# Sums of three weight quads moved into the last pair's attention, x's tiles loaded ahead on another queue, one pair's outputs kept in SBUF

## The chip, the cores and the metric

The kernel runs on one core of a Trainium2 chip. The metric is device time of one execution in microseconds; the median of several runs is given. The engines are named as in the profile: PE (TensorE, matrix products; PEld is its weight load), DVE (VectorE), ACT (ScalarE), POOL (GpSimd) and SP (SyncE, which only issues transfers). Transfers are issued on SP's, ACT's or POOL's queue, and each queue issues in its own order: what waits at its head holds what stands behind it. Accumulating transfers (`accum_op=ALU.add`) are all issued by POOL here.

## The reference

One decoder layer, 1024 tokens by 1024 features, all in float32:

```
proj = rms_norm(h, g1) @ w_in
a_b, a_c, a_h, q, k, v, c_u, c_v = split(proj)
y_a = a_b * short_conv(a_c * a_h)                     # width 256
y_b = stick_breaking_attention(norm(q), norm(k), v)   # 8 heads of 64
y_c = spatial_gating(gelu(c_u), gelu(c_v))            # width 256
h = h + concat(y_a, y_b, y_c) @ w_out
f = square(relu(rms_norm(h, g2) @ w_ff1))             # 1024 x 4096
h = h + f @ w_ff2
h = h + sigmoid(rms_norm(h, g3) @ w_ple_gate) * (p @ w_ple_proj)
```

## The kernel before

**Layout.** Activations are kept transposed, features on the 128 partitions, tokens along the row, in two halves of 512 tokens. Each float32 operand of a matrix product is split into a high and a low part (`split`, L135: a rounding copy on ACT, L138, and a subtraction on DVE, L139), and each product is three matmuls (L165 to L167; L772 in the later stages): high times high, high times low, low times high. SBUF tiles of 128 x 512 come from a pool of 56 slots (`slot`) and from smaller pools of the later stages (`late_slot`: 4 tiles "raw", 6 "sum", 22 "w", 12 "tmp").

**Order.** The program text doesn't fix the order in which instructions go into an engine's queue. A planner makes it when the program is built: it plays the program through with a timing model and issues on each engine what is ready, earlier text first. `with tc.issue_after(x)` only forbids that what stands in the block is queued ahead of `x` on x's engine. At run time each engine works in the order of its queue and waits on semaphores.

**Stages.** First come the projections, the spatial gating and the attention. The eight heads are worked in four pairs (`attend(pr)`, eight steps each: a head of the pair and a group of 256 queries; `stick` makes the weights, `gather` turns them and multiplies by v). Beside a pair's attention `weave` runs a stream of other products: the projections of the next pairs, and in the last pair the convolution (`convolve`), whose last part is left for after the attention. In `stick`, POOL multiplies the weights of query blocks 0, 1, 2, 4 and 6 (L429), DVE the others; `last_pool` and `last_act` name the latest such instruction on POOL and the latest sigmoid on ACT. In `convolve`, POOL scales u (L603) and the sum (L613), and DVE evicts the last product from PSUM (L615).

The attention's outputs of pairs 0 to 2 go to HBM (`y_dram`, rows 0 to 2). The last pair's are gathered in two tiles `y_b`, each stored to row 3 when it is full (L490). The gating's outputs are rows 4 and 5; the convolution's stay in SBUF (`y_a`, rows 6 and 7). `bring(0)` loads and splits the rows of the first token half ahead of the next stage; the second half's are loaded within it.

**The stage of w_out** (L879 to L928) runs over two token halves and eight row blocks each, in the order 0, 4, 1, 5, 2, 6, 3, 7. Each block is 24 matmuls into a PSUM bank `o_ps`. Its weights come as two loads "raw" on SP's queue (except in the first two blocks, whose weights are brought early); x's tile `xt` follows on SP's queue (L898; the last two by `fetch`). DVE adds the product to x (L758), ACT's queue stores the sum (`h_dram`), ACT scales it by the gain (L911, `hg`) and squares it (L845), and the squares are added up, in the first half on POOL (L758), in the second by an accumulating transfer (L849). The scaled sums are split as operands `hn` of the next stage. The root of the first half's mean square goes over DVE (`diag`, L866) to PE (`R_ps`, L873).

**The first feed-forward product** multiplies 2 x 2 blocks by seven products in place of eight. Its weights are 16 quads of blocks A11, A12, A21 and A22 (each 128 x 512 floats), and needs four sums of each: S1 = A21 + A22, S2 = A11 + S1, S3 = A11 + A21, S4 = A12 + S2. For quads 3 to 15 these are made in SBUF as the stage goes. For the first three (`EARLY`) they are made in HBM, in `u_sums`, in twelve steps, four for each quad (`block_step`, L745): in step 0 S1 and S3 get a copy of a block, in step 1 S1 gets A22 added and S2 a copy of A11, in step 2 S3 gets A21 and S2 gets S1 added, in step 3 S4 gets a copy of A12 and then S2 added. Copies are issued on ACT's queue (L752), additions on POOL's (L750). The twelve steps stand in the stage of w_out, one for each block whose squares are added up (`up_sums`), queued behind that addition and behind the scaling L911. SP's queue loads the sums from `u_sums` in the second half of the stage.

The weights of the second feed-forward product are summed likewise, in `w_sums`, in 32 steps over the four pairs' attention (`block_sums`, L287); in the last pair only one transfer of these is left. The rest of the kernel, both feed-forward products and the gate, the change doesn't touch.

Of the kernel before, what the change touches and what calls it, by code (L numbers as in the profile page):

```python
# [7 lines left out]
F32 = mybir.dt.float32  # L8
F32R = mybir.dt.float32r
AF = mybir.ActivationFunctionType  # L10
# [22 lines left out]
def hybrid_block(ctx: ExitStack, tc: tile.TileContext, a: dict):  # L33
# [39 lines left out]
    def halves(s, dt=F32, shape=(P, HT)):  # L73
        return [slot(s, dt, shape) for _ in range(2)]
# [212 lines left out]
    def block_sums(i, behind):  # L287


        with tc.issue_after(behind[0].ins), tc.issue_after(behind[1].ins):  # L290
            for to, what in PASSES[i % 4]:
# [12 lines left out]
                else:  # L304
                    nc.scalar.dma_start(w_sums[to, rows], src[rows])

    last_pool, last_act = [None], [None]
    summed = []
    heads = {}
    y_dram = dram.tile([6, 2, P, HT], F32, name="y_dram")  # L310

    def project(pr):
# [77 lines left out]
    def attend(pr):  # L390

        QS, KH, KL, V, _ = heads[pr]
        yb = halves("y_b") if pr == 3 else None
        weights, both, seen_g = {}, [None], []

        def store_rows():
# [39 lines left out]
        def gather(hh, g):  # L436
            own = slice(hh * HD, (hh + 1) * HD)
            wts = weights.pop((hh, g))
            av_of[0] ^= 1
            av = av_bank[:, av_of[0] * 256:(av_of[0] + 1) * 256]  # L440

            def turn(j):

                tr = bank(ps_tr, "w_tr")
                n = 0
                parts = []
                for kb in (2 * j, 2 * j + 1):
                    first = 0 if kb <= 2 * g else 1
                    parts.append((kb, n, first))
                    for i in range(first, 2):  # L450
                        nc.tensor.transpose(tr[:, n:n + P], wts[i][:, kb * P:(kb + 1) * P], ident)  # L451
                        n += P
                hi, lo = tmp("wT_hi", F32R), tmp("wT_lo", F32R)
                split(tr[:, :n], hi[:, :n], lo[:, :n])
                return parts, hi, lo, n // P

            turned = []
            for j in range(-2, g + 1):
                if j + 2 <= g:
                    turned.append(turn(j + 2))  # L460
                    yield 2 * turned[-1][3] + 10
                if j < 0:
                    continue
                parts, hi, lo, _ = turned.pop(0)
                for kb, o, first in parts:
                    m = 256 - first * P
                    lhs = V[kb // 2][:, kb % 2, hh].rearrange("p two d -> p (two d)")
                    for part in (hi, lo):
                        nc.tensor.matmul(av[:, first * P:], lhs, part[:, o:o + m],  # L469
                                         start=kb == 0 and part is hi,  # L470
                                         stop=kb == 2 * g + 1 and part is lo)
                yield 8

            if yb is None:
                if both[0] is None:
                    both[0] = slot("y_both")
                t = both[0]
                nc.scalar.copy(t[:, (g % 2) * 256:(g % 2 + 1) * 256], av)
                if len(seen_g) % 2:
                    nc.gpsimd.dma_start(t[:HD], t[HD:], accum_op=ALU.add)  # L480
                    summed.append((y_dram[pr, g // 2, own], t))
                    both[0] = None
                seen_g.append(g)
                return
            low = half_tmp("av_lo")
            nc.scalar.copy(low[:HD], av[HD:])
            nc.vector.tensor_tensor(out=yb[g // 2][own, (g % 2) * 256:(g % 2 + 1) * 256],
                                    in0=av[:HD], in1=low[:HD], op=ALU.add)
            if hh == 1 and g % 2 == 0:
                nc.sync.dma_start(y_dram[pr, g // 2], yb[g // 2])  # L490

        steps = [(0, g) for g in range(4)] + [(1, g) for g in reversed(range(4))]
        yield from stick(*steps[0])
        for i, step in enumerate(steps):
            if i + 1 < len(steps):
                yield from stick(*steps[i + 1])
            block_sums(8 * pr + i, (last_pool[0], last_act[0]))
            yield from gather(*step)
            if i % 2 == 1:
                store_rows()  # L500
# [155 lines left out]
        weave(attend(pr), ATTEND, fill, PROJECT if pr < 3 else CONVOLVE * 0.72)  # L656
    y = [[], []]

    def bring(h):

        i = len(y[h])
        src = stage(y_dram[i, h]) if i < 6 else y_a[i - 6][h]
        y[h].append(pair("y"))
        split(src, *y[h][-1])

    def early_units(src):

# [9 lines left out]
    for i in range(7):  # L677
        bring(0)
        if i in (2, 4):
            first_wu[2 * i - 4] = early_units(a["w_out"][2 * i - 4])  # L680
        for _ in take(fill, CONVOLVE * 0.28 / 7):
            pass
    for _ in fill:
        pass
    bring(0)
# [42 lines left out]

    OPERAND = {1: "A11", 2: "A12", 4: "A22", 5: "S1", 6: "S2", 7: "S3", 3: "S4"}

    def w_block(key, of, *at):
        return a[key][(2 * (int(of[1]) - 1) + int(of[2]) - 1, *at)]

    def down_operand(p, c, j):
        of = OPERAND[p]
        if of[0] == "A":
            return w_block("w_ff2", of, c, j)
        s = w_sums[int(of[1]) - 1].rearrange("r n -> (r n)")
        return s.rearrange("(c j p n) -> c j p n", j=4, p=P, n=2 * HT)[c, j]


    STEPS = [((0, "A21"), (2, "A11")), ((0, "+A22"), (1, "A11")), ((2, "+A21"), (1, "+S1")),
             ((3, "A12"), (3, "+S2"))]

    def block_step(step, sums, blocks, copies):  # L745
        for to, what in STEPS[step]:
            of = what.strip("+")
            src = sums(int(of[1]) - 1) if of[0] == "S" else blocks(of)
            if what[0] == "+":
                nc.gpsimd.dma_start(sums(to), src, accum_op=ALU.add, max_dma_last_dim=2048)  # L750
            else:
                copies.dma_start(sums(to), src)  # L752

    def subtract(eng, out, x, y):
        return eng.tensor_tensor(out=out, in0=x, in1=y, op=ALU.subtract)
# [23 lines left out]
    UP = (1, 6, 5, 7, 2, 3, 4)  # L779
    FIRST = (1, 2, 6, 5, 7, 3, 4)  # L780
    raw_of, up_pairs = {}, {}

    EARLY = 3
    u_sums = dram.tile([EARLY, 4, P, HT], F32, name="u_sums")

    def up_sums(i, behind_add, behind_act):

        if i < 4 * EARLY:
            with tc.issue_after(behind_add.ins), tc.issue_after(behind_act.ins):
                block_step(i % 4, lambda to: u_sums[i // 4, to],  # L790
                           lambda of: w_block("w_ff1", of, i // 4), nc.scalar)

    def load_up(q, to, of):
        tag = "sum" if to[0] == "S" else "raw"
        src = u_sums[q, int(of[1]) - 1] if of[0] == "S" else w_block("w_ff1", of, q)
# [80 lines left out]
    def hn_pair(src):  # L876
        return two_parts(src, lambda s: slot(f"hn_{s}", F32R))

    last_sqs, up_step = [], [0]  # L879
    late_bank("pass"), late_bank("pass")  # L880
    for h in range(2):
        for n in (0, 4, 1, 5, 2, 6, 3, 7):
            end = h == 1 and n in (3, 7)
            if h == 1:

                if n == 5:
                    with tc.issue_after(block_end.ins):
                        diag = root_of([S2[0]], "20")
                elif n == 6:
                    with tc.issue_after(block_end.ins):  # L890
                        spread_root(diag, R2[0])
                supply({4: -12, 1: -10, 5: -8, 2: -6, 6: -4, 7: -3}.get(n, -100))
            wu = first_wu[n] if h == 0 and n in first_wu else plain_units(a["w_out"][n])
            if end:
                xt = fetch(a["xT"][n * P:(n + 1) * P, half[h]], "sum")
            else:
                xt = slot("xt")
                nc.sync.dma_start(xt, a["xT"][n * P:(n + 1) * P, half[h]])  # L898
            o_ps = late_bank("o_ps")
            block_end = product(o_ps, [(wu[k], y_parts[h][k]) for k in range(KT)])  # L900
            if h == 0:
                i = len(y_parts[1])
                src = fetch(y_dram[i, 1], "sum") if i < 6 else y_a[i - 6][1]
                y_parts[1].append(two_parts(src, lambda s: late_slot("w", f"y_{s}", F32R)))
            if h == 1 and n == 7:
                supply(-0.975)

            evicted = add(nc.vector, xt, o_ps, xt)
            nc.scalar.dma_start(h_dram[n, h], xt)
            t = hg[n][h] = late_slot("tmp", "hg")  # L910
            scaled = nc.scalar.activation(t, xt, AF.Copy, scale=g2[:, n:n + 1])  # L911
            summed = late_squares(S2[h], xt, n == 0, h == 1, end)
            if end:
                last_sqs.append(summed)
            elif summed:
                up_sums(up_step[0], summed, scaled)
                up_step[0] += 1
            if h == 1 and n == 7:
                supply(-0.955)
            j = n % 4  # L920
            if h == 0:
                hn[1 if n < 4 else 2][j] = hn_pair(t)
            elif n >= 4:
                b11, b12, b21 = hg[j][0], hg[j][1], hg[n][0]
                t2 = late_slot("tmp", "t2")
                token_sums(b11, b12, b21, t, nc.vector, b11, t2, b12, b21)
                for p, src in ((6, t2), (5, b11), (7, b12), (3, t), (4, b21)):
                    hn[p][j] = hn_pair(src)  # L928
# [374 lines left out]
```

## Time and profile before

| | us |
|---|---|
| median of 3 runs (1233.39 to 1236.79) | 1236.44 |
| the profiled execution | 1236.95 |
| its span, from the first instruction to the last | 1234.4 |
| PE busy in the span | 1201.2 |
| DVE busy | 885.5 |
| ACT busy | 627.4 |
| POOL busy | 393.3 |

Times in the profile count from the start of the span. The last pair's attention with the convolution beside it runs from about 345 us to 424.7, the stage of w_out from there to about 530, the first feed-forward product to about 840, the second to about 1147, and then the gate. The page cuts the span into 40 slices of 30.9 us; a digit is the busy share in tenths. A matmul's end is modelled, so a busy PE can still run at half its clock; the granted clock stands in a column of its own. A wait is put down to the instruction whose end released it.

### The profile page before, as it was taken

The numbers are of one execution on the slowest core, as the hardware profiler recorded it, in microseconds if no ns is written. First come the engines' busy times: TensorE is split into PE (matmuls) and PEld (weight loads), VectorE is DVE, ScalarE is ACT, GpSimd is POOL, SyncE is SP. The second block draws the span as 40 slices with busy tenths as digits, with TensorE's granted clock in tenths as the row PEclk, the third lists the DMA queues.
The fourth block names the chain that finished last, engine by engine and source line by source line (L and its number), as shares of the span: only waits on it lengthen the run. The fifth ranks groups of instructions, "written<-read, shape, count | busy, mean of one in ns | idle before, by whom it ended". The sixth has DMA issues, their size and how long they took to land.

```text
span 1234.4 us, 17751 instructions
## 1 busy us (share of the span) xinstructions
PE 1201.2 (97%) x5852; PEld 1027.2 (83%) x5852; DVE 885.5 (72%) x1310; ACT 627.4 (51%) x1244; POOL 393.3 (32%) x408
## 2 busy tenths in 40 slices
PE   9999999999999998899999999999999999999997
PEld 7899899898988787688888888888888888888886
DVE  7746888879689654787787777777755566753597
ACT  7726666667565353553433433445544344555552
POOL 2324345355222222215445345331013211013412
PEclk9999999999999998999999999999999999999999
DMA  9602359998621378989999998868969985653957
GB/s 315 217 18 101 113 164 263 244 188 148 129 70 35 116 236 251 265 240 242 267 254 239 259 265 224 255 206 283 363 212 306 298 257 183 200 180 104 185 158 211
DMA packets 128539, 255.08 MB, mean 207 GB/s; under 512 B 14560, under 2 KB 22496, under 8 KB 127744
## 3 DMA queue, kind: packets, MB, share of 16 engines
q1 hardware_dynamic: 97584, 172.80, 42.1%
q0 software_dynamic: 27664, 57.05, 24.7%
q10 hardware_dynamic: 3200, 24.12, 5.3%
q8 instruction: 46, 0.75, 0.3%
q14 instruction: 45, 0.37, 0.1%
HBM read 192.83 MB, written 93.32 MB: 232 GB/s over the span
## 4 chain that ended last, share of the span: by engine, by line
PE 84%; DVE 6%; DMA 4%; issue 2%; ACT 2%; POOL 1%; SPq 0%; ACTq 0%; DVEq 0%; POOLq 0%
PE f_ps L772 25%; PE d_ps L772 25%; PE g_ps L772 6%; PE qkv_ps L165 3%; PE qkv_ps L166 3%; PE qkv_ps L167 3%; DMA xt<-in_xT 2%; PE av L469 2%; DVE rem L426 2%; PE w_tr L451 2%; PE cv_ps L165 1%; PE cv_ps L166 1%; PE cv_ps L167 1%; PE vu_ps L167 1%; PE vu_ps L165 1%
## 5 line engine op out<-in xcount | busy, mean ns | idle before, releaser
L139 DVE TENSOR_TENSOR w_lo<-raw,w_hi 128x512 fp32r<-128x512 f32 x280 | 239.8, 860 | 83.5 <-ACT w_hi L138 80.8
L138 ACT CAST w_hi<-raw 128x512 fp32r<-128x512 f32 x280 | 171.5, 619 | 230.0 <-PE d_ps L772 106.8
L772 PE MATMUL f_ps<-hn_hi,w_hi 128*128 128x512 f32 x448 | 175.5, 393 | 0.0
L772 PE MATMUL f_ps<-hn_lo,w_hi 128*128 128x512 f32 x448 | 175.3, 391 | 0.0
L772 PE MATMUL f_ps<-hn_hi,w_lo 128*128 128x512 f32 x448 | 175.0, 391 | 0.0
L772 PE MATMUL d_ps<-f_hi,w_hi 128*128 128x512 f32 x448 | 174.8, 390 | 0.0
L772 PE MATMUL d_ps<-f_hi,w_lo 128*128 128x512 f32 x448 | 174.3, 389 | 0.0
L772 PE MATMUL d_ps<-f_lo,w_hi 128*128 128x512 f32 x448 | 174.3, 389 | 0.0
L426 DVE TENSOR_TENSOR_SCAN rem<-rem 128x128 f32<-128x128 f32 (+3 forms) x64 | 91.7, 1438 | 19.5 <-ACT rem L421 18.7
L772 PEld LDWEIGHTS f_ps<-hn_hi,w_lo 128*128 128x128 f32 x448 | 84.8, 189 | 17.9
L772 PEld LDWEIGHTS f_ps<-hn_hi,w_hi 128*128 128x128 f32 x448 | 84.8, 189 | 17.7 <-issue 0.2
L772 PEld LDWEIGHTS f_ps<-hn_lo,w_hi 128*128 128x128 f32 x448 | 84.7, 189 | 17.9 <-issue 0.2
L772 PEld LDWEIGHTS d_ps<-f_hi,w_hi 128*128 128x128 f32 x448 | 84.1, 188 | 17.7 <-issue 0.2
L772 PEld LDWEIGHTS d_ps<-f_lo,w_hi 128*128 128x128 f32 x448 | 84.1, 188 | 17.7 <-issue 0.2
L772 PEld LDWEIGHTS d_ps<-f_hi,w_lo 128*128 128x128 f32 x448 | 84.1, 188 | 17.3
L165 PE MATMUL qkv_ps<-whi,xn_hi 128*128 128x384 f32 x256 | 92.6, 362 | 1.9 <-DVE V L142 1.8
L166 PE MATMUL qkv_ps<-wlo,xn_hi 128*128 128x384 f32 x256 | 89.7, 350 | 0.0
L167 PE MATMUL qkv_ps<-whi,xn_lo 128*128 128x384 f32 x256 | 89.5, 350 | 0.0
L139 DVE TENSOR_TENSOR f_lo<-raw,f_hi 128x512 fp32r<-128x512 f32 x112 | 77.1, 719 | 12.2 <-ACT f_hi L138 11.7
L138 ACT CAST f_hi<-raw 128x512 fp32r<-128x512 f32 x112 | 67.1, 620 | 28.5 <-DMA raw<-f_dram 25.5
L758 POOL TENSOR_TENSOR S<-S,sq 128x512 f32<-128x512 f32 x19 | 27.4, 1440 | 170.1 <-ACT sq L845 170.1
L429 POOL TENSOR_TENSOR wt<-wt,rem 128x127 f32<-128x127 f32 (+4 forms) x40 | 45.3, 1141 | 83.2 <-DVE rem L426 43.8
(250 smaller groups left out, 2709.1 us busy)
## 6 DMA issues: line engine op xcount, KB each, us to landing
raw<-in_w_ff SPq DMA_DIRECT2D x148, 256.0 KB, 4.1
raw<-f_dram SPq DMA_DIRECT2D x112, 256.0 KB, 5.1
raw<-w_sums SPq DMA_DIRECT2D x64, 256.0 KB, 4.2
f_dram<-f SPq DMA_DIRECT2D x48, 256.0 KB, 4.0
f_dram<-t SPq DMA_DIRECT2D x48, 256.0 KB, 3.7
w_sums<-in_w_ff POOLq DMA_DIRECT2D x8, 1024.0 KB, 11.7
w_sums<-w_sums POOLq DMA_DIRECT2D x8, 1024.0 KB, 12.5
raw<-in_w_out SPq DMA_DIRECT2D x28, 256.0 KB, 4.3
```

Of the source, the lines that this page charges most:

```text
L138: last_hi[0] = nc.scalar.copy(hi, src)
L139: low.tensor_tensor(out=lo, in0=src, in1=hi, op=ALU.subtract)
L165: nc.tensor.matmul(ps, lh, rh, start=first and i == 0, stop=False)
L166: nc.tensor.matmul(ps, lh, rl, start=False, stop=False)
L167: done = nc.tensor.matmul(ps, ll, rh, start=False, stop=last and i == len(terms) - 1)
L426: nc.vector.tensor_tensor_scan(out=back, data0=back, data1=back, initial=1.0, op0=ALU.mult, op1=ALU.bypass)
L429: done = (nc.vector if on_vector else nc.gpsimd).tensor_tensor(out=wt[:, :W - 1], in0=wt[:, :W - 1], in1=rem[:, 1:W], op=ALU.mult)
L451: nc.tensor.transpose(tr[:, n:n + P], wts[i][:, kb * P:(kb + 1) * P], ident)
L469: nc.tensor.matmul(av[:, first * P:], lhs, part[:, o:o + m], start=kb == 0 and part is hi, stop=kb == 2 * g + 1 and part is lo)
L758: return eng.tensor_tensor(out=out, in0=x, in1=y, op=ALU.add)
L772: done = nc.tensor.matmul(bank, l, r, start=first and k == 0 and i == 0, stop=k == len(b) - 1 and i == 2, skip_group_check=True)
```

## The change

There are three parts.

1. The twelve steps of `up_sums` are called elsewhere: one in each of the eight steps of the last pair's attention, and one in each of the first four rounds of the loop that brings the rows of y. Each is queued behind the latest weight product on POOL and, on ACT, behind the latest sigmoid or, in the loop, the latest copy of `bring`. `STEPS`, `block_step`, `w_block` and `u_sums` move up in the text, unchanged.
2. The tiles `xt` of all blocks but the last two are loaded from ACT's queue, three ahead of the block that uses them.
3. The last pair's two tiles of outputs are kept (`y_kept`) and split from there; row 3 is neither stored nor loaded. The rows are brought, and multiplied, in the order 0, 1, 2, 4, 5, 6, 3, 7.

```diff
+    EARLY = 3
+    u_sums = dram.tile([EARLY, 4, P, HT], F32, name="u_sums")
+    up_step = iter(range(4 * EARLY))
+
+    def up_sums(behind_add, behind_copy):
+
+        i = next(up_step, None)
+        if i is not None:
+            with tc.issue_after(behind_add.ins), tc.issue_after(behind_copy.ins):
+                block_step(i % 4, lambda to: u_sums[i // 4, to],
+                           lambda of: w_block("w_ff1", of, i // 4), nc.scalar)
+
...
+    y_kept = []
...
@@ attend @@
-        yb = halves("y_b") if pr == 3 else None
+        yb = y_kept if pr == 3 else None
+        if pr == 3:
+            y_kept.extend(halves("y_b"))
...
-            if hh == 1 and g % 2 == 0:
-                nc.sync.dma_start(y_dram[pr, g // 2], yb[g // 2])
...
             block_sums(8 * pr + i, (last_pool[0], last_act[0]))
+            if pr == 3:
+                up_sums(last_pool[0], last_act[0])
             yield from gather(*step)
...
+    ORDER = (0, 1, 2, 4, 5, 6, 3, 7)
+
+    def kept(i, h):
+        return y_kept[h] if i == 3 else y_a[i - 6][h] if i > 5 else None
+
     def bring(h):
 
-        i = len(y[h])
-        src = stage(y_dram[i, h]) if i < 6 else y_a[i - 6][h]
+        i = ORDER[len(y[h])]
+        src = kept(i, h)
+        src = stage(y_dram[i, h]) if src is None else src
         y[h].append(pair("y"))
         split(src, *y[h][-1])
+        last_act[0] = last_hi[0]
...
         for _ in take(fill, CONVOLVE * 0.28 / 7):
             pass
+        up_sums(last_pool[0], last_act[0])
...
@@ the stage of w_out @@
-    last_sqs, up_step = [], [0]
+    last_sqs = []
+    tiles = [(h, n) for h in range(2) for n in (0, 4, 1, 5, 2, 6, 3, 7)]
+    to_bring, x_of = iter(tiles), {}
+
+    def bring_x():
+
+        h, n = next(to_bring, (1, 3))
+        if h == 1 and n in (3, 7):
+            return
+        x_of[h, n] = slot("xt")
+        nc.scalar.dma_start(x_of[h, n], a["xT"][n * P:(n + 1) * P, half[h]])
+
+    for _ in range(3):
+        bring_x()
...
-                xt = slot("xt")
-                nc.sync.dma_start(xt, a["xT"][n * P:(n + 1) * P, half[h]])
+                xt = x_of.pop((h, n))
+                bring_x()
             o_ps = late_bank("o_ps")
-            block_end = product(o_ps, [(wu[k], y_parts[h][k]) for k in range(KT)])
+            block_end = product(o_ps, [(wu[i], y_parts[h][k]) for k, i in enumerate(ORDER)])
             if h == 0:
-                i = len(y_parts[1])
-                src = fetch(y_dram[i, 1], "sum") if i < 6 else y_a[i - 6][1]
+                i = ORDER[len(y_parts[1])]
+                src = kept(i, 1)
+                src = fetch(y_dram[i, 1], "sum") if src is None else src
...
-            elif summed:
-                up_sums(up_step[0], summed, scaled)
-                up_step[0] += 1
```

More of the change, by code (lines that the diff above doesn't have):

```diff
@@ L305, in block_sums, with w_block, block_step @@
                     nc.scalar.dma_start(w_sums[to, rows], src[rows])
+    def w_block(key, of, *at):
+        return a[key][(2 * (int(of[1]) - 1) + int(of[2]) - 1, *at)]
+    STEPS = [((0, "A21"), (2, "A11")), ((0, "+A22"), (1, "A11")), ((2, "+A21"), (1, "+S1")),
+             ((3, "A12"), (3, "+S2"))]
+    def block_step(step, sums, blocks, copies):
+        for to, what in STEPS[step]:
+            of = what.strip("+")
+            src = sums(int(of[1]) - 1) if of[0] == "S" else blocks(of)
+            if what[0] == "+":
+                nc.gpsimd.dma_start(sums(to), src, accum_op=ALU.add, max_dma_last_dim=2048)
+            else:
+                copies.dma_start(sums(to), src)
+    EARLY = 3
[7 more added lines that the diff above has]
+                           lambda of: w_block("w_ff1", of, i // 4), nc.scalar)
     last_pool, last_act = [None], [None]
@@ L739, in down_operand @@
         return s.rearrange("(c j p n) -> c j p n", j=4, p=P, n=2 * HT)[c, j]
[L742 to L752, printed above, removed]
     def subtract(eng, out, x, y):
@@ L781, in hybrid_block @@
     raw_of, up_pairs = {}, {}
[L783 to L791, printed above, removed]
     def load_up(q, to, of):
@@ L910, in hybrid_block @@
             t = hg[n][h] = late_slot("tmp", "hg")
-            scaled = nc.scalar.activation(t, xt, AF.Copy, scale=g2[:, n:n + 1])
+            nc.scalar.activation(t, xt, AF.Copy, scale=g2[:, n:n + 1])
             summed = late_squares(S2[h], xt, n == 0, h == 1, end)
```

2 lines of the change are left out of this document (removed).

## The prediction

> **What bounds the kernel now.** I read the page's 40 slices first, for where TensorE (PE) is not full.
>
> ```profile
> PE   9999999999999998899999999999999999999997
> ```
>
> The two 8s are slices 15 and 16, 463 to 525 us of the span: the stage that multiplies by w_out and leads into the first feed-forward product. Next I asked for busy time by stretches. The columns are: length; busy time and number of instructions of PE, PEld, DVE, ACT and POOL; granted TensorE clock; DMA share; GB/s.
>
> ```profile
> 117.00:345.00 228.00, 215.88 (x1329) 203.28 (x1328) 187.53 (x286) 150.11 (x379) 103.28 (x102) 0.96 0.73 181
> 345.00:424.70 79.70, 79.70 (x437) 68.08 (x435) 62.90 (x82) 37.66 (x84) 22.52 (x17) 1.00 0.20 49
> 424.70:428.00 3.30, 0.56 (x3) 0.47 (x3) 2.62 (x5) 2.45 (x4) 0.00 (x0) 1.00 1.01 317
> ...
> 471.00:482.00 11.00, 7.42 (x21) 5.58 (x20) 3.81 (x5) 3.52 (x6) 1.28 (x1) 0.69 0.91 278
> ...
> 505.00:509.00 4.00, 2.43 (x9) 1.39 (x8) 2.58 (x4) 1.76 (x3) 0.85 (x1) 1.00 0.98 265
> ...
> 519.00:526.00 7.00, 4.17 (x14) 3.02 (x12) 4.41 (x8) 5.15 (x10) 2.60 (x3) 0.76 0.99 254
> 526.00:546.00 20.00, 20.00 (x102) 17.01 (x101) 18.36 (x31) 14.89 (x28) 1.73 (x2) 1.00 0.88 239
> 424.70:546.00 121.30, 110.58 (x480) 90.12 (x480) 80.06 (x122) 68.66 (x122) 24.50 (x25) 0.96 0.88 254
> ```
>
> Length minus PE busy gives four gaps: 2.74, 3.58, 1.57 and 2.83 us, together 10.72; that is all of the last row (121.30 - 110.58). Two gaps are followed by a clock under 1.00: (1 - 0.69) x 11 = 3.4 us and (1 - 0.76) x 7 = 1.7 us of lost clock, of which I take off 0.6 as falling inside the gaps: 4.5 us. So at most 10.7 + 4.5 = **15.2 us** can be won in this stage. Ahead of it, in the last pair's attention (345 to 424.7), PE is full and DMA is 0.20 busy: room, but nothing to win.
>
> Who ends the gaps is in PE's waits between 425 and 555 us (total, times, longest) and in the chain of waits:
>
> ```profile
> PE o_ps L167 <- DVE w_lo L139: 3.6, 1, 3.6
> PE o_ps L165 <- ACT w_hi L138: 2.8, 1, 2.8
> PE o_ps L165 <- DVE cv_acc L615: 2.7, 1, 2.7
> PE R_ps L873 <- DVE diag L866: 1.6, 1, 1.6
> ```
>
> ```profile
> 419.49 2.32 DMA y_dram<-y_b
> ...
> 422.39 2.96 DMA stage<-y_dram
> ...
> 426.69 0.69 DVE cv_acc L615
> 427.51 0.47 PE o_ps L165
> ...
> 459.60 7.67 DMA u_sums<-u_sums
> ...
> 468.18 5.80 DMA xt<-in_xT
> ...
> 474.62 0.69 DVE w_lo L139
> ...
> 501.91 4.38 DMA xt<-in_xT
> ...
> 506.92 0.69 DVE diag L866
> ...
> 514.18 5.66 DMA xt<-in_xT
> 519.87 0.70 DVE xt L758
> ...
> 522.11 0.61 ACT w_hi L138
> ```
>
> The reader is to see three kinds of late transfer. First gap: y_b goes out to HBM and back (2.32 + 2.96), its split holds DVE, and the PSUM eviction L615 behind it on DVE holds PE. Second: an accumulation into u_sums lands 7.67 us after its issue; SyncE's queue stands at the load of that sum, and x's tile behind it is issued only at 468.18. Third and fourth: x's tile is late, L758 waits for it on DVE, and diag, hg and w_hi queue behind L758.
>
> **The change part by part.** *y_b kept on chip.* Removed: two stores and two loads. On SyncE's queue:
>
> ```profile
> 404.63 15.19 SPq L490 DMA_DIRECT2D y_dram<-y_b  x2
> 421.96 0.80 SPq L66 DMA_DIRECT2D stage<-y_dram  x2
> ```
>
> Nothing was issued between the two stores, nor behind the second until it had landed; y rows 4 and 5, w_out's second early block and the first loads of the new stage stood behind it. They can now go earlier. Row 3 moves to seventh place in the product; its source is written by 419.49, and its two conversions (0.61 on ACT, 0.69 on DVE, by the rows of w_hi and w_lo) fit ahead of 424.7. L615 can start when PE's last convolution matmul ends at 424.8: 0.69, plus the 0.13 by which PE followed it, plus a hand-off, leaves 0.9 us of the 2.74. Gain 1.8. The two tiles stay longer in the 56 slots; xn's 32 slots come free at that moment, so I count nothing; without that cover a split of an early y waits for a slot, under 1 us.
>
> *x's tiles on ScalarE's queue, three ahead.* 14 DMAs leave SyncE's queue:
>
> ```profile
> L898 SPq DMA_DIRECT2D xt<-in_xT x14: 376/450/1777, 424.8 to 514.2; - x14
> ```
>
> 14 x 0.45 = 6.3 us of issue move to ScalarE, which is busy 68.66 of 121.30 us: covered. Three blocks ahead is 72 matmuls of 0.23 us (110.58 / 480 in the stage's row), 16.6 us, against 5.8 us of landing. A DMA that waited for its slot would hold ScalarE's scalings and splits behind it, and PE behind those; the price would be a gap like those of today (1.6 to 3.6 us), but with 32 slots just freed I take nothing.
>
> *The sums made earlier.* 24 DMAs move from 443 to 534 us into the attention and the convolution's end:
>
> ```profile
> L752 ACTq DMA_DIRECT2D u_sums<-in_w_ff x12: 496/520/729, 443.2 to 521.0; - x12
> L750 POOL DMA_DIRECT2D u_sums<-in_w_ff x6: 790/810/1216, 453.4 to 523.8; - x6
> L750 POOL DMA_DIRECT2D u_sums<-u_sums x6: 809/990/1168, 459.6 to 533.8; - x6
> ```
>
> They take 12 x 0.52 = 6.2 us on ScalarE and 6 x 0.81 + 6 x 0.99 = 10.8 us on GpSimd, which in 345 to 424.7 are busy 37.66 and 22.52 of 79.70. What they free in the DMA engines follows from the queues of 424 to 546 us (packets, MB, share of 16 engines):
>
> ```profile
> q0 software_dynamic: 2448, 4.46, 23.6%
> q10 hardware_dynamic: 2688, 7.34, 16.6%
> ```
>
> q0's share is 28.8 us for 4.46 MB, q10's 20.3 us for 7.34 MB; by bytes, 3.15 MB on each are 20.3 and 8.7 us. So 29 of 0.88 x 121.3 = 107 us of DMA time leave the stage, and its share falls to about 78 / 106 = 0.74. Gap two's cause goes, and the queue that made x late thins as well: gaps two and four go with their clock (3.58 + 2.83 + 4.5 = 10.9).
>
> What it costs the attention isn't in this trace. Below: nothing, as PE there is never short of work. Above: the stretch of the earlier pairs, which carries the like sums for w_ff2 (L302, L305), loses 228 - 215.88 = 12.1 us idle and 0.04 x 228 = 9.1 us of clock; at that rate 79.7 us would lose 7.4. I take 1.0, near the stage's own row (0 idle), because the earlier loss also has the projections' waits in it.
>
> What is late next: DVE. From 526 to 546 it is busy 18.36 of 20 us, and with less waiting ahead of it the stage becomes denser. For that I leave one gap the size of the third, 1.6.
>
> *Sum:* 15.2 - 0.9 - 1.6 - 1.0 = 11.7 us. The profiled execution took 1236.95 us (span 1234.4 and 2.55 around it); 1236.95 - 11.7 = 1225.3. The median shown, 1236.44, is 0.5 under that execution: **1225** in round numbers.
>
> On the clock: a 2.83 us gap was followed by 0.76, while after the 2.74 us gap the clock stayed 1.00. The Trainium skill, "TensorE: Matmul & The Clock Gate", Part 1, lowers the clock only after an idle window of about 3.4 us; by that rule the fourth gap would cost no clock, and the gain would be 1.4 less, 1226 to 1227. The trace has the lowered clock, and the sum goes by it.
>
> **The rivals.** *A, transfers stay the limit.* DMA share is 0.98 to 0.99 in both late gaps, and x only changes its queue. If x still lands late there, the third and fourth gaps stay (1.57 + 2.83 + 1.4 = 5.8, of which 1.6 is in the sum): 4.2 more, 1229. Against it: the 29 us that leave. The Trainium skill, "DMA: Bandwidth & Descriptors", section "Issuing engines are not separate DMA queues", says that starting transfers from several engines saves only issue time, since all share 16 DMA engines; that speaks against the move of x, though not against an earlier issue. This trace can't separate the two.
>
> *B, DVE becomes the bound* of the second half: 80.06 of 121.30 us is little, 18.36 of 20 is not. w_lo would come late where x did before: the same gaps, the same 1229.
>
> *C, slower: GpSimd's queue.* Each step's accumulation needs an earlier one landed, and GpSimd works in order:
>
> ```profile
> 468.40 0.81 POOL L750 DMA_DIRECT2D u_sums<-u_sums  x1 [4.41 <-DMA u_sums<-in_w_ff]
> ```
>
> ```profile
> 402.28 0.64 POOL L429 TENSOR_TENSOR wt<-wt,rem 128x255 f32<-128x255 f32 x1 [0.72 <-DVE rem L426]
> ...
> 416.04 1.30 POOL L603 TENSOR_TENSOR cv_u<-cv_u,R 128x512 f32<-128x512 f32 x1 [1.83 <-DVE cv_u L602]
> 420.55 1.29 POOL L613 TENSOR_TENSOR cv_acc<-cv_acc,R 128x512 f32<-128x512 f32 x1 [3.21 <-DVE cv_acc L611]
> ```
>
> ```profile
> u_sums<-in_w_ff POOLq DMA_DIRECT2D x6, 256.0 KB, 4.9
> u_sums<-u_sums POOLq DMA_DIRECT2D x6, 256.0 KB, 7.5
> ```
>
> Steps 6 to 11, counted from 0, all hang on the attention's last weight product, 402.3 to 402.9. They have seven accumulations, 6.3 us to issue at 0.9, and wait on GpSimd for three landings in a row, those of steps 6, 9 and 10: 7.5 + 4.9 + 7.5. That ends at 429. If the convolution's L603 is queued behind them, L613 ends 5.8 us after L603's start, at 435, and L615 frees PE at 436 instead of 425.7: 10.3 us, and 2.9 of clock after such a gap: 1238. With the attention at its upper bound (6.4 more) it is 1244; I put C at 1241. It decides from where GpSimd holds L603 past 416 by more than the convolution's slack (L613's end at 421.8 to PE's 424.8: 3 us). Against it: the DMA engines are nearly idle there, so landings should be shorter, and the planner, which models landings, can put L603 first.
>
> *D, the steps come late.* The call only forbids an earlier issue; if the planner puts the last steps into w_out's stage all the same, the second gap with its clock stays (3.58 + 3.1): 1232.
>
> **How the numbers follow.** Forecast 0.50, its own range 1221 (all 15.2 won) to 1228; A 0.10, B 0.14; D 0.09; C 0.17. A change under 0.3%, 3.7 us, can't be told from none: faster means under 1232.7, slower over 1240.1. Faster: 0.50 + 0.24 + 0.04 of D = 0.78. Same: 0.05 of D and 0.05 of C, whose weaker form ends at 1238: 0.10. Slower: 0.12. The range goes from 1220, the full gain less the runs' scatter, to 1237, past D and short of most of C.
>
> **What would show it.** Right: L898 on ScalarE's queue, no late x among DVE's waits; u_sums written by 430 and loaded without a wait; SyncE free between 405 and 420; PE idle in the stage near 2.5 us and its clock near 1.00; PE still full from 345 to 425. Wrong: PE gaps in the last pair's attention or ahead of the first o_ps, ended by POOL or by L615; PE waiting for w_lo behind hn_lo on DVE; DMA share still above 0.9.

## The result, and the profile after

The changed kernel takes 1221.12 us (median of 4 runs, 1218.53 to 1223.13) against 1236.62 for the kernel before in the same runs: a ratio of **0.9873, interval 0.9847 to 0.9899**, or 15.5 us less. The profiled execution took 1223.13 us, with a span of 1221.2: 13.8 and 13.2 us less than the one of before. Timed again later, the same kernel gave 1221.11 and a ratio of 0.9873 (0.9842 to 0.9903). The prediction was 1225 in a range of 1220 to 1237.

The page's PE row, 40 slices:

```profile
PE   9999999999999999999999999999999999999997
```

The two 8s are gone. The stretches that the prediction showed of before, in the changed kernel (length; busy time and number of instructions of PE, PEld, DVE, ACT, POOL; granted clock; DMA share; GB/s):

```profile
345.00:424.70 79.70, 79.70 (x430) 68.15 (x429) 63.26 (x78) 39.34 (x86) 29.20 (x26) 0.98 0.53 118
424.70:428.00 3.30, 2.75 (x13) 1.99 (x12) 3.30 (x6) 1.49 (x3) 2.13 (x2) 1.00 0.53 66
...
471.00:482.00 11.00, 10.69 (x46) 8.18 (x45) 7.19 (x9) 6.16 (x12) 2.59 (x2) 1.00 0.69 221
...
505.00:509.00 4.00, 4.00 (x19) 3.34 (x18) 2.62 (x5) 2.50 (x5) 0.00 (x0) 1.00 0.54 141
...
519.00:526.00 7.00, 7.00 (x33) 5.79 (x32) 6.19 (x11) 4.78 (x9) 0.00 (x0) 1.00 0.79 263
```

Where PE stood 2.74, 3.58, 1.57 and 2.83 us, it now stands 0.55, 0.31, 0 and 0, and the clock of the two slowed stretches is 1.00 in place of 0.69 and 0.76. DMA share in the attention went from 0.20 to 0.53 (the sums are made there now).

The stage ends earlier, so the same window holds later work at its end. For a comparison that holds I take the stage from the end of the convolution's last matmul to the end of the second `R_ps`, and for each kernel the one row of that stretch. Before:

```profile
424.78:554.00 129.22, 118.51 (x505) 96.26 (x506) 86.47 (x133) 69.82 (x124) 26.84 (x27) 0.95 0.88 252
```

After, with the row of the piece ahead of it, and the row behind it to the end of the span:

```profile
320.00:425.87 105.87, 104.02 (x562) 88.24 (x560) 82.03 (x114) 55.00 (x124) 38.17 (x38) 0.98 0.59 130
425.87:540.80 114.93, 114.07 (x505) 93.28 (x506) 86.23 (x132) 67.75 (x118) 20.06 (x16) 0.99 0.71 222
540.80:1221.20 680.40, 672.26 (x3001) 557.18 (x2999) 467.21 (x648) 300.31 (x513) 203.81 (x208) 1.00 0.80 234
```

The stage holds the same 505 matmuls and is 129.22 - 114.93 = **14.3 us** shorter: 10.71 - 0.86 = 9.85 us of idle time and 4.4 of clock. It starts 425.87 - 424.78 = 1.1 us later. What follows takes 680.40 us in both. 14.3 - 1.1 = 13.2, the difference of the spans; nothing is left over.

PE's waits from 320 to 560 us in the changed kernel, all three (total, times, longest):

```profile
PE cv_ps L165 <- DVE cv_u L632: 1.9, 1, 1.9
PE o_ps L165 <- DVE cv_acc L647: 0.5, 1, 0.5
PE o_ps L167 <- DVE w_lo L139: 0.3, 1, 0.3
```

The first lies in the attention, at 342 us; it is what the change costs there. x's tiles and the last kind of step, by tile (duration ns min/median/max; first and last start):

```profile
L902 ACTq DMA_DIRECT2D xt<-in_xT x14: 334/335/492, 426.4 to 490.1; - x14
```

```profile
L319 POOL DMA_DIRECT2D u_sums<-u_sums x6: 805/828/1108, 369.9 to 424.8; - x6
```

The last x tile is issued at 490.1 in place of 514.2, the last accumulation at 424.8 in place of 533.8: all twelve steps have left the stage.

### The profile page after: what moved, and what is told of

It is laid out like the page before. It is cut to its first block, busy times and chain, and to the rows that moved or that the text cites. A ratio compares the mean times of both kernels' runs of the same rounds, so it can differ in the third digit from the quotient of the medians.

```text
span 1221.2 us, 17746 instructions
## 1 busy us (share of the span) xinstructions
PE 1197.3 (98%) x5852; PEld 1023.5 (84%) x5852; DVE 882.6 (72%) x1310; ACT 629.0 (52%) x1244; POOL 395.7 (32%) x408
## 4 chain that ended last, share of the span: by engine, by line
PE 84%; DVE 7%; DMA 3%; issue 2%; ACT 2%; POOL 1%; SPq 0%; ACTq 0%; DVEq 0%; POOLq 0%
PE f_ps L796 25%; PE d_ps L796 25%; PE g_ps L796 6%; PE qkv_ps L165 3%; PE qkv_ps L166 3%; PE qkv_ps L167 3%; DVE rem L458 2%; PE av L501 2%; PE w_tr L483 2%; PE cv_ps L165 2%; PE cv_ps L166 2%; PE cv_ps L167 2%; PE vu_ps L165 1%; PE vu_ps L167 1%; PE vu_ps L166 1%
## 5 line engine op out<-in xcount | busy, mean ns | idle before, releaser
L139 DVE TENSOR_TENSOR w_lo<-raw,w_hi 128x512 fp32r<-128x512 f32 x280 | 236.7, 849 | 82.3 <-ACT w_hi L138 80.4
L458 DVE TENSOR_TENSOR_SCAN rem<-rem 128x128 f32<-128x128 f32 (+3 forms) x64 | 92.6, 1454 | 16.0 <-ACT rem L453 15.5
```

The source lines that it names most:

```text
L139: low.tensor_tensor(out=lo, in0=src, in1=hi, op=ALU.subtract)
L458: nc.vector.tensor_tensor_scan(out=back, data0=back, data1=back, initial=1.0, op0=ALU.mult, op1=ALU.bypass)
```

## The experiments

Each of the three parts alone and each taken out of the whole, then x's move taken apart, then the cost in the attention. "Idle", "clock" and "DMA" are those of the stage, by a row like the ones above; times in us.

| kernel | median | ratio (interval) | stage | PE idle | clock | DMA |
|---|---|---|---|---|---|---|
| before | 1236.62 | 1 | 129.2 | 10.7 | 0.95 | 0.88 |
| after | 1221.12 | 0.9873 (0.9847 to 0.9899) | 114.9 | 0.9 | 0.99 | 0.71 |
| after_again | 1221.11 | 0.9873 (0.9842 to 0.9903) | 114.8 | 0.9 | 0.99 | 0.72 |
| only_y | 1234.86 | 1.0005 (0.9985 to 1.0025) | 126.0 | 9.2 | 0.97 | 0.86 |
| only_sums | 1224.21 | 0.9915 (0.9883 to 0.9947) | 116.2 | 2.8 | 1.00 | 0.76 |
| only_x | 1223.22 | 0.9905 (0.9868 to 0.9943) | 118.5 | 4.4 | 0.99 | 0.94 |
| no_x | 1226.13 | 0.9926 (0.9900 to 0.9953) | 115.6 | 2.8 | 1.00 | 0.70 |
| no_y | 1226.89 | 0.9927 (0.9907 to 0.9948) | 119.9 | 3.5 | 0.97 | 0.74 |
| no_sums | 1222.49 | 0.9909 (0.9886 to 0.9932) | 120.0 | 3.8 | 0.97 | 0.89 |
| x_sp | 1222.97 | 0.9900 (0.9880 to 0.9919) | 114.1 | 0.6 | 0.99 | 0.68 |
| x_act0 | 1224.48 | 0.9907 (0.9881 to 0.9933) | 115.1 | 2.5 | 1.00 | 0.71 |
| only_x_sp | 1223.25 | 0.9898 (0.9866 to 0.9929) | 118.3 | 3.9 | 0.99 | 0.94 |
| only_x_act0 | 1234.25 | 0.9991 (0.9966 to 1.0015) | 133.0 | 13.3 | 0.94 | 0.85 |
| late_start | 1226.45 | 0.9923 (0.9896 to 0.9950) | 119.4 | 5.9 | 0.92 | 0.69 |

The kernel before had medians of 1234.16 to 1235.77 beside the experiments, single runs between 1228 and 1243; a ratio is against the runs on the same chip. What follows the stage took 680.4 to 680.8 us in every profiled execution. The start of the stage lies between 418.6 and 427.7, in executions whose granted clock ahead of 320 us differs; so mechanisms are read from the stage, and the worth of a kernel from its ratio. Each stage is that of one execution: of only_x_act0 it is the slowest of ten (1238.97), of only_y the fastest of twelve (1233.13). The changed kernel alone was profiled twice: 114.9 and 114.8.

**Theory:** each part closes gaps of its own: y the first, the sums the second, x the third and fourth. The prediction was less clear-cut: its sum lets the fourth go with the sums, its rivals A and D divide the gaps as here. **Rivals:** the sums alone suffice, since all late transfers come from their traffic; x alone suffices, since only x is late; x's new queue gives nothing.

### One part alone

**only_y**, parts 1 and 2 undone in the changed kernel:

```diff
-            if pr == 3:
-                up_sums(last_pool[0], last_act[0])
...
+            elif summed:
+                up_sums(summed, scaled)
...
-                xt = x_of.pop((h, n))
-                bring_x()
+                xt = slot("xt")
+                nc.sync.dma_start(xt, a["xT"][n * P:(n + 1) * P, half[h]])
```

> The kernel before with part 3 alone: y_b kept, rows in the new order. Theory of three separate causes: the first gap (2.74 us) shrinks to about 0.6, the three later gaps stay as they are; 1.8 to 2.2 us less than before, about 1234.6. Rival, the stage is paced by transfers: it starts earlier but meets the same late transfers, a later gap grows by what the first loses, and the time stays at 1236.6.

**only_sums**, parts 2 and 3 undone (x as in only_y):

```diff
-        yb = y_kept if pr == 3 else None
+        yb = halves("y_b") if pr == 3 else None
...
+            if hh == 1 and g % 2 == 0:
+                nc.sync.dma_start(y_dram[pr, g // 2], yb[g // 2])
...
-    ORDER = (0, 1, 2, 4, 5, 6, 3, 7)
+    ORDER = (0, 1, 2, 3, 4, 5, 6, 7)
```

> The kernel before with part 1 alone: the twelve steps moved into the last pair's attention. Three separate causes: the second gap with its clock goes (6.7 us), the attention costs 1.1, the first gap and the two at x's tiles stay; about 1231. Rival, traffic: the 24 transfers were also what made x late, so the gaps at x go as well; about 1225 to 1226, and x lands in time though it is still issued from SyncE's queue.

**only_x**, parts 1 and 3 undone by the edits above; x stays three ahead on ScalarE's queue:

```diff
-        up_sums(last_pool[0], last_act[0])
...
-    ORDER = (0, 1, 2, 4, 5, 6, 3, 7)
+    ORDER = (0, 1, 2, 3, 4, 5, 6, 7)
...
+            elif summed:
+                up_sums(summed, scaled)
```

> The kernel before with part 2 alone: x three ahead on ScalarE's queue. Three separate causes: the third and fourth gaps with their clock go (5.8 us), the second stays, because w_out's weights still stand on SyncE's queue behind the load of u_sums; about 1231. Rival, the order of SyncE's queue is all there is: with x off that queue the second gap goes too; about 1224 to 1225. Rival, traffic: x lands late all the same, nothing gained; 1236.

The stage's row of only_y, of only_sums and of only_x, in this order:

```profile
424.33:550.30 125.97, 116.80 (x505) 94.29 (x506) 83.18 (x128) 67.00 (x117) 27.01 (x27) 0.97 0.86 245
```

```profile
424.79:540.99 116.20, 113.39 (x506) 91.70 (x505) 86.78 (x133) 69.41 (x124) 17.97 (x16) 1.00 0.76 234
```

```profile
424.10:542.63 118.53, 114.17 (x505) 93.41 (x506) 85.56 (x133) 69.92 (x124) 28.16 (x27) 0.99 0.94 276
```

Against 129.22 they are shorter by 3.3, 13.0 and 10.7 us: 27.0 together, where the whole change gives 14.3. So the parts don't add up: **the sums and x are two remedies for the same gaps**, and either alone gives about 1% (0.9915 and 0.9905).

Kept y alone gives nothing that can be told from no change: 1.0005, with an interval that reaches down to 0.9985, 1.9 us less. PE's waits of only_y:

```profile
PE o_ps L167 <- DVE w_lo L139: 5.0, 3, 3.4
PE o_ps L165 <- ACT w_hi L138: 2.4, 2, 1.2
PE o_ps L165 <- DVE cv_acc L645: 1.6, 1, 1.6
```

The first gap falls from 2.7 to 1.6, and the waits behind it stay: 7.4 us in all, where before had 8.0. The transfers there are still late. In this execution the stage is even 3.3 us shorter; that the time doesn't fall with it is not explained, but a gain of the 1.1 us that the first gap lost would lie within the interval.

only_x refutes what the prediction built on the second gap, that it stays as long as the sums are made in the stage. SyncE still waits for the sums, in total 8.0 us (10.1 before), and w_out's loads behind them come late to ACT; but PE waits only 1.1 and 0.7 us for weights. Waits of SyncE, of ACT and of PE in only_x:

```profile
SPq L738 <- DMA u_sums<-u_sums: 8.0, 2, 5.8
```

```profile
ACT w_hi L138 <- DMA raw<-in_w_out: 7.6, 4, 4.8
```

```profile
PE o_ps L165 <- DVE cv_acc L645: 2.6, 1, 2.6
PE o_ps L167 <- DVE w_lo L139: 1.1, 1, 1.1
PE o_ps L165 <- ACT w_hi L138: 0.7, 1, 0.7
```

The 3.58 us were the price of x standing behind the load of the sum, not of the sum or of the weights. Nor did the traffic alone make it late: at a DMA share of 0.94, above that of before, an x tile took longer to land (median 5.4 us, 4.6 before), and still came in time because it was asked for early.

How the sums alone get there is seen in DVE's waits for x between 425 and 541 us. Before:

```profile
DVE xt L758 <- DMA xt<-in_xT: 19.6, 10, 8.3
```

In only_sums, where x is issued as before:

```profile
DVE xt L782 <- DMA xt<-in_xT: 5.0, 4, 2.0
DVE w_lo L139 <- DMA xt<-in_xT: 2.2, 1, 2.2
```

x isn't asked for earlier than in its own block, but no load of a sum holds the queue for more than 2.2 us (6.6 before), and the share fell to 0.76. Which of the two counts there, the freer queue or the thinner traffic, these runs don't separate.

### One part taken out

**no_x**, x loaded in its own block from SyncE's queue:

```diff
-    for _ in range(3):
-        bring_x()
...
-                xt = x_of.pop((h, n))
-                bring_x()
+                xt = slot("xt")
+                nc.sync.dma_start(xt, a["xT"][n * P:(n + 1) * P, half[h]])
```

> The changed kernel with x's tiles back on SyncE's queue, one block at a time. Three separate causes: the two gaps at x come back, 4 to 6 us over the changed kernel, 1225 to 1227. Rival, traffic: with the sums gone x is in time anyway; within 1 us of the changed kernel, 1221 to 1222.

**no_y**, part 3 undone, the two others left:

```diff
+                nc.sync.dma_start(y_dram[pr, g // 2], yb[g // 2])
...
+    ORDER = (0, 1, 2, 3, 4, 5, 6, 7)
```

> The changed kernel with the last pair's outputs stored to HBM and loaded again, rows in the old order. Three separate causes: the first gap is back at 2.7 us, about 2 us over the changed kernel, 1223. Rival: without the sums' traffic and with x elsewhere the queue catches up within the first blocks; no difference, 1221.

**no_sums**, the steps back in the stage:

```diff
-        up_sums(last_pool[0], last_act[0])
...
+            elif summed:
+                up_sums(summed, scaled)
```

> The changed kernel with the twelve steps back in the stage of w_out, one for each block. Three separate causes: the second gap with its clock is back (6.7 us) and the attention's 1.1 us is saved: about 1227. Rival, traffic: the sums crowd the stage and x and the weights are late again all through it: 1230 or more. Rival, x's head start was enough: 1221 to 1222.

Without x's move the stage is 0.6 us longer, without the sums' 5.1, without kept y 5.0. In idle time that is 2.0, 2.9 and 2.6 us more; the rest is clock, which even went the other way in no_x. So y, which alone shows nothing, is worth about as much as the sums once the others are done; neither forecast for no_y, 2 us or none, was near it.

It isn't the first gap that comes back in no_y: ahead of the stage's first products PE stands 0.45 and 0.23 us, and 0.35 a little later. Its longest wait comes later, at 446.46, and the clock from 446 to 452 us is 0.72:

```profile
PE o_ps L165 <- ACT w_hi L138: 2.2, 1, 2.2
```

The chain of waits leads from there to a row of y, issued at 438.70 and landed 5.50 us later. SyncE's queue begins late in no_y: the first weights of w_out that aren't brought early are issued at 430.18, in the changed kernel at 426.32.

With no_x the runs are some 0.5% behind the whole change, more than 0.6 us; in its profiled execution another 1.8 us lie ahead of the stage (427.65 against 425.87). Whether that part belongs to the edit is left open.

In no_x, DVE still waits for x 8 times, 13.5 us in all, yet PE is idle only 2.8:

```profile
DVE xt L782 <- DMA xt<-in_xT: 13.5, 8, 3.3
```

The longest single wait, 3.3, says more than the total: with longest waits of 2.0 to 3.3 (only_sums, x_act0, no_x) PE stood 2.5 to 2.8 us, with 4.5 to 8.3 (only_y, only_x_act0, before) 9.2 to 13.3. That fits a lead of PE over DVE that swallows some 3 us at a time. It was not tested by itself, and the three with short waits are also the three with the sums moved.

### Queue or head start

**x_sp**, and **only_x_sp** with parts 1 and 3 undone as well: three ahead, from SyncE's queue.

```diff
-        nc.scalar.dma_start(x_of[h, n], a["xT"][n * P:(n + 1) * P, half[h]])
+        nc.sync.dma_start(x_of[h, n], a["xT"][n * P:(n + 1) * P, half[h]])
```

> The changed kernel with x's tiles still asked for three blocks ahead, but on SyncE's queue. If the head start is what counts, it is as fast as the changed kernel, 1221. If leaving SyncE's queue is what counts, x stands behind w_out's loads, which wait for the four raw tiles, and lands late: 1225 or more.

> The kernel before with x asked for three blocks ahead, still on SyncE's queue; sums and y as before. If the head start is what counts, the stage of w_out is as short as with x on ScalarE's queue, about 118 us, and the time near 1224. If the queue is what counts, x still stands behind the load that waits for u_sums, the second gap stays, and the stage is 125 us or more.

**x_act0**, and **only_x_act0** with parts 1 and 3 undone as well: from ScalarE's queue, each tile in its own block.

```diff
-    for _ in range(3):
-        bring_x()
...
-                xt = x_of.pop((h, n))
-                bring_x()
+                bring_x()
+                xt = x_of.pop((h, n))
```

> The changed kernel with x's tiles on ScalarE's queue, but each asked for only in its own block. If the queue is what counts, 1221 to 1222: ScalarE can issue while its block's matmuls run, and 5.5 us cover a landing of about 4. If the head start is what counts, DVE waits for x in many blocks: 1225 or more.

> The kernel before with x on ScalarE's queue, each tile asked for only in its own block; sums and y as before. If the queue is what counts, the stage is about 118 us. If the head start is what counts, x lands late under the sums' traffic in many blocks, the late gaps stay, and the stage is 122 us or more.

With the sums in the stage the answer is clear: three ahead on SyncE's old queue gives 0.9898, the new queue without the head start 0.9991, no change. In the latter the gaps stand as before or worse; PE's waits, and DVE's for x:

```profile
PE R_ps L883 <- DVE diag L876: 4.8, 1, 4.8
PE o_ps L167 <- DVE w_lo L139: 4.4, 2, 3.5
PE o_ps L165 <- DVE cv_acc L645: 2.7, 1, 2.7
PE o_ps L165 <- ACT w_hi L138: 1.4, 1, 1.4
```

```profile
DVE xt L779 <- DMA xt<-in_xT: 18.1, 9, 5.1
```

**With the sums in the stage it is the head start that counts, not which engine's queue.** In only_x_sp SyncE still waits for the sums, at most 4.8 us at a time, but the tile behind that wait is one for three blocks (16.6 us) later:

```profile
SPq L738 <- DMA u_sums<-u_sums: 6.9, 2, 4.8
```

The new queue isn't a free one either. In only_x_act0 ACT stores a block's sum at 451.32, scales and squares it, and only then, at 452.51, issues the next block's x, which DVE then waits for until 457.69. So x stands there behind work that has itself waited for the x of the block ahead.

The Trainium skill, "DMA: Bandwidth & Descriptors", section "Issuing engines are not separate DMA queues", says that another issuing engine saves only the time of issue, as all share the same 16 DMA engines; only_x from ScalarE's queue and only_x_sp from SyncE's agree (0.9905 and 0.9898). With the sums moved, x_sp and x_act0 differ by what the runs can't tell apart (0.9900 and 0.9907; stages 114.1 and 115.1).

### The cost in the attention, and the kernel again

PE's idle time from 320 us to the stage is 0.59 before (104.78 long, 104.19 busy) and 1.85 after (105.87 - 104.02). It is one place. DVE's order of time, before:

```profile
343.37 0.69 DVE L600 TENSOR_TENSOR cv_u<-cv_ps,R 128x512 f32<-128x512 f32 x1
343.98 1.22 DVE L426 TENSOR_TENSOR_SCAN rem<-rem 128x512 f32<-128x512 f32 x1
```

And after:

```profile
340.59 1.22 DVE L458 TENSOR_TENSOR_SCAN rem<-rem 128x512 f32<-128x512 f32 x1
...
342.74 0.69 DVE L632 TENSOR_TENSOR cv_u<-cv_ps,R 128x512 f32<-128x512 f32 x1
```

The planner, with other work to place, put the wide scan of 1.22 us ahead of the eviction that frees the convolution's bank, and PE waits 1.9 in place of 0.6. The profiles of all six kernels with the steps in the stage have the 0.6 there, all seven profiles with the steps begun where the change begins them the 1.9. **late_start** begins the steps one step of the attention later; **after_again** is the changed kernel without an edit.

```diff
-            if pr == 3:
+            if pr == 3 and i:
                 up_sums(last_pool[0], last_act[0])
```

> The changed kernel with the twelve steps begun one step later in the last pair's attention (seven there, five in the loop). The planner's order on DVE then has cv_u's eviction ahead of the wide scan again, as before the change. If that swap is what the attention paid, PE's wait for cv_u falls from 1.9 to 0.6 us and no lowered clock follows it; 1.3 to 3.4 us under the changed kernel, the stage of w_out unchanged at about 115 us. Rival, the transfers themselves cost the attention: PE's wait moves elsewhere and nothing is won.

> The changed kernel itself, once more beside the others on one chip: about 0.987 of the kernel before, its stage of w_out near 115 us. It shows how far the front of the kernel moves from run to run with the granted clock.

late_start has the old order there, but not the gain. Its PE waits:

```profile
PE o_ps L165 <- ACT w_hi L138: 5.9, 1, 5.9
PE w_tr L483 <- DVE wt L461: 1.7, 1, 1.7
PE cv_ps L165 <- DVE cv_u L632: 0.6, 1, 0.6
```

The wait for cv_u is 0.6 again, but a new one of 1.7 stands at 383 us, still in the attention: PE is idle 103.92 - 101.66 = 2.26 us from 320 us to the stage, more than the 1.85 of the changed kernel. So the wait moved elsewhere and nothing was won, as the rival had it; whether the transfers or the new order moved it, this run doesn't show. And a gap of 5.9 opened at the start of the stage. The chain of waits there:

```profile
423.95 4.54 DMA raw<-y_dram
...
428.56 0.62 ACT y_hi L138
429.18 0.61 ACT w_hi L138
429.81 0.77 PE o_ps L165
```

A row of y lands late, and ACT's split of it and of a weight come ahead of the first `o_ps`. That product reads early weights and an early row (`y_hi`, `wo_hi`); why it was queued behind this work was not found, and stays open. What the run does show: a small shift of the steps changes the whole order at this border, by more than the cost it was to remove.

No kernel here beats the changed one. only_x_sp comes nearest with the least: the head start for x alone, everything else as before, gives 0.9898, and its interval overlaps that of the whole change.

## Why the prediction was right, point by point

The time was right (1225 forecast, 1221.1 measured), and so was the sum on the stage; **the attribution of gaps to parts was wrong.**

**The sum.** Forecast for the stage was 15.2 - 0.9 - 1.6 = 12.7; it gave 14.3. The 4.5 us of clock were 4.4. The start kept 0.55 us of its gap in place of 0.9. The residual gap of 1.6 that I left for a denser DVE was 0.31: this term was mis-sized, and of the 2.2 us by which the profiled execution lies under the sum's 1225.3, 1.3 are in it. Outside the span 1.93 us took the place of 2.55, which the sum didn't have. The other 2.0 us, from 1223.13 to the median, are scatter: the profiled execution was the slowest of the four.

**y_b kept, "gain 1.8".** The gap went from 2.74 to 0.55 in the whole change, but kept y alone closes it only to 1.6 (only_y, and no_sums too), and the time shows nothing (1.0005). The sums' move, which the prediction didn't count here, takes its share: with y stored and the sums moved PE stands 1.2 us at the start of the stage in only_sums and 1.0 in no_y. How, stays open. And inside the whole change kept y is worth more than its gap: 2.6 us of idle time, most of it in a later wait.

**"Gap two's cause goes" with the sums.** This step failed. The reading was right, a sum lands late, SyncE's queue stands at its load, and x's tile is issued behind it; the conclusion was not, that the sum had to go, and that without it the gap stays (rival D, 1232). only_x showed that with x asked for early the same late sums cost PE 1.8 us for weights in the whole stage, where gaps two to four had 8.0. The sums' move closes these gaps too (1.6 left in only_sums), so beside x it is worth less than the 10.9 it was given. no_sums, which is D's case, waits for no weights longer than 1.2 us, has a stage 5.1 us longer than the whole change's, 2.9 of it idle, and ran in 1222.5.

**x, three ahead on ScalarE.** Right that its head start is enough; the queue, the other half of that step, gave nothing.

**DMA time, "0.88 to 0.74".** It came to 0.71. Queues from 424 to 541 us after (packets, MB, share of 16 engines):

```profile
q10 hardware_dynamic: 4320, 7.87, 18.6%
q0 software_dynamic: 987, 1.82, 9.3%
```

q0 fell from 4.46 MB to 1.82 and from 23.6% to 9.3%, 28.8 us to 10.9, where 8.5 was reckoned; q10 rose from 16.6% to 18.6%, since the copies left it and x's 14 tiles came. But share wasn't what bound PE: only_x has 0.94 with 4.4 us idle, only_x_act0 0.85 with 13.3.

**The attention, 1.0.** Measured 1.1 between the two profiled executions, with 1.26 us more of idle time. That the two figures agree is luck: the mechanism was another one than the traffic that I bounded it by, a changed order on DVE, and in the second profile of the changed kernel the stage starts at 424.89, 0.1 us later than before, with the same idle time.

**The rivals.** A fell: no x is late in the changed kernel. B fell: DVE is busy 86.23 of 114.93 us, and PE's only wait for w_lo is 0.3. D fell: all steps lie ahead of 425. C's mechanism was there without its price. POOL's order of time, and DVE's:

```profile
410.86 0.81 POOL L319 DMA_DIRECT2D u_sums<-u_sums  x1 [4.85 <-DMA u_sums<-u_sums]
411.41 1.57 POOL L635 TENSOR_TENSOR cv_u<-cv_u,R 128x512 f32<-128x512 f32 x1
```

```profile
407.90 0.69 DVE L634 TENSOR_TENSOR cv_u<-cv_ps,cv_u 128x512 f32<-128x512 f32 x1 [1.00 <-PE cv_ps L167]
413.77 0.75 DVE L643 SCALAR_TENSOR_TENSOR cv_acc<-cv_u,c_conv_w,cv_acc 128x511 f32<-128x511 f32 x1 [5.18 <-ACT cv_acc L636]
```

The same DVE instruction in the kernel before:

```profile
409.87 0.75 DVE L611 SCALAR_TENSOR_TENSOR cv_acc<-cv_u,c_conv_w,cv_acc 128x511 f32<-128x511 f32 x1 [2.17 <-ACT cv_acc L604]
```

L635 had its input at 407.90 + 0.69 = 408.59 and ran at 411.41: 2.8 us behind an accumulation that stood for a landing, as C had it, and DVE behind it stood 5.18 in place of 2.17. But one landing stood ahead of L635, not three in a row (the last accumulation, which waited 3.40 us for a landing, was issued at 424.83, behind both L635), and 3.0 us just fit into the slack of 3 us that C was given: PE waited 0.5 for the eviction L647, not 10.3.

**A sign that came out otherwise.** I had SyncE free between 405 and 420. It stands at two of w_out's loads from 402.56 for 12.93 us:

```profile
402.56 12.93 SPq L66 DMA_DIRECT2D stage<-in_w_out  x2
```

It cost nothing that PE shows.

## What to carry to other kernels

Where a transfer is late because its queue stands at another one, ask for it some blocks ahead before thinning the traffic or changing the queue: here that one edit gave 1.0%, and a new queue without it, behind that engine's own work, nothing. The gaps of a stage are not a list of separate debts: the parts alone shortened the stage by 3.3, 13.0 and 10.7 us and together by 14.3, so test a part by taking it out of the whole as well as by putting it in alone. At each late transfer in a chain of waits ask whether it would still hold the engine if only it were asked for early: the prediction named both the sum and the x tile behind it, but took moving the sum for necessary, and asking early for x was enough.

## What the hardware showed beside this

**The clock after short gaps.** In the changed kernel the gap of 1.85 us at 342 us was followed by half the clock; two microseconds of it:

```profile
346.00:348.00 2.00, 2.00 (x7) 1.52 (x6) 0.00 (x0) 0.00 (x0) 0.00 (x0) 0.50 0.29 66
```

The same kernel's second profiled execution has the same gap, and after it:

```profile
346.00:348.00 2.00, 2.00 (x11) 1.65 (x10) 0.61 (x2) 0.00 (x0) 0.00 (x0) 1.00 0.15 33
```

Seven of the profiled executions have this gap of 1.85 us: three show 0.50 two to three us after it (the changed kernel's first, x_sp, x_act0), four 1.00 (its second, only_sums, no_x, no_y). So the same gap is followed by a lowered clock in one execution and not in another; in the kernel before, 2.74 us was followed by 1.00 and 2.83 by 0.76. The Trainium skill, "TensorE: Matmul & The Clock Gate", Part 1, gives an idle window of about 3.4 us that runs freely; that it is not tied to the gaps would fit these executions, but a gap of 1.85 is shorter than a window of that length, and the measurement decides.

**A granted clock of 0.95 that costs nothing.** In late_start's profile the clock stands at 0.95 for the whole rest; a stretch of it:

```profile
560.00:700.00 140.00, 140.00 (x619) 115.93 (x618) 112.01 (x119) 50.62 (x87) 65.97 (x63) 0.95 0.95 258
```

The same stretch of the changed kernel:

```profile
560.00:700.00 140.00, 140.00 (x619) 115.94 (x618) 104.03 (x118) 52.69 (x90) 65.82 (x61) 1.00 0.93 254
```

619 matmuls in 140 us in both, and 680.48 us for the rest against 680.40. A clock of 0.50 shows in the number of matmuls (7 against 11 above); 0.95 here doesn't, so a granted clock is to be believed only where the count of matmuls goes with it.
